# Delta rule: TensorE's program order from longer assumed times for keys, GpSimd's rows and the transposition

## The chip, the cores and the metric

The kernel runs on one core of a Trainium2 chip. The metric is the device time of one execution in microseconds, lower is better. TensorE (PE) multiplies, VectorE (DVE), ScalarE (ACT) and GpSimd (POOL) work on the vectors, and SyncE (SP) issues nearly all transfers.

## The reference

A decoder trunk of four layers on 256 tokens of width 1024. Each layer adds a mixer and a convolutional feed-forward part to the residual stream. The mixers are block attention (layers 0 and 3), a short convolution (layer 1) and a gated delta rule (layer 2, 8 heads of 128). The delta rule is what the change touches:

```python
proj = h @ w_in
qkv = silu(causal_dwconv(proj[..., :3 * d], conv_w))
q = l2norm(q) * (dh ** -0.5);  k = l2norm(k)
a_mat = where(strict, einsum('bhnid,bhnjd->bhnij', k_beta, k) * decay, 0.0)
t_mat = triangular_solve(a_mat + eye, eye)          # per head and chunk
u = t_mat @ v_beta;  w = t_mat @ (k_beta * exp(gc)[..., None])
attn = where(incl, einsum('bhnid,bhnjd->bhnij', q, k) * decay, 0.0)
def step(state, inp):
    v_new = u_i - w_i @ state
    o_i = q_i @ state + a_i @ v_new
    state = state * sd_i[..., None, None] + einsum('bhck,bhcv->bhkv', k_i, v_new)
o = rmsnorm(o) * norm_w * silu(z);  return o @ w_o
```

## The kernel before

**Weights.** All weights come in one stream of 128x1024 chunks. SyncE loads a chunk (`wraw`, L128), ScalarE rounds it (`whi`, L150), VectorE takes the remainder (`wlo`, L151). Each block of a projection is three TensorE products of 128x256, all at line L252 with an output named `mm`. The small products of the delta rule also stand at L252, their transpositions at L255, both with an output named `sm` (four PSUM banks in turn).

**The delta rule.** Projections run in the order of `GDN_FILL`: queries with keys of heads 0 to 7 (q0 to q7), then values (v0 to v3, two heads each) and gates (z0 to z3). Between them runs the work of two halves, heads 0 to 3 and heads 4 to 7. For each half: `lengths` transposes queries and keys and squares them; `systems` multiplies keys with keys and queries (`sm<-yqk`), scales the result into `aq` on VectorE (L733), and stores it to DRAM (L741); `invert` reloads its 16-row blocks (`bl`, L756), inverts them row by row on GpSimd (L764 to L769), stores the result (L771) and reloads it (`xc`, L774); VectorE spreads it (`xt`, L777) and transposes it (`xi`, L784, in `turn`); `join16` and two `join_half` put the blocks together on TensorE; `solve`, `scores` and `finish` make the output, which `output` gates and splits into two parts (L983, then ScalarE L413, VectorE L414). Then `residual` multiplies with the output weights, in the order of `PLAN_HALVES`: for all eight blocks first the part of heads 0 to 3, then that of heads 4 to 7. It needs the mark `o0` for the first and `o1` for the second.

**The order on TensorE** is written while the program is built. `Weave` counts model time: each block of a projection costs `TILE`, and each step of the small work yields its cost and how long to wait, or the marks to wait for. A step is put into TensorE's program at the first place in the projections at which its wait has passed by the model. The model delays nothing on the chip; it only decides the order. The waits that matter here:

```python
wv.set(f"q{h}", L_QK)      # queries_keys: from SiLU to the transpositions
yield 0, L_JOIN            # invert: from GpSimd's start to join16
yield 0, L_XI              # join16: behind each turn(s)
wv.set(f"o{s.h0 // G_H}", L_OUT)
```

TensorE keeps the order so written. The orders of VectorE, ScalarE, GpSimd and SyncE come out of a scheduler at build time that starts from the same program. Every engine has one static order.

Of the kernel before, what the change touches and what calls it, by code (L numbers as in the profile page):

```python
# [36 lines left out]
TILE = 0.327  # L37
LAG = 1.75
L_HEAD, L_SOFTMAX, L_TURN, L_MIX, L_READY = 3.5, 9.0, 1.0, 2.5, 0.5
L_QK, L_V, L_LEN, L_SYS, L_BLOCKS, L_JOIN, L_XI, L_PM, L_OUT = 6.0, 6.0, 1.0, 0.5, 6.0, 13.0, 1.0, 2.5, 1.0  # L40


PV_MIX = 0
# [1068 lines left out]
```

## Time and profile before

| what | value |
|---|---|
| median of 3 runs | 1251.23 us (1249.75 to 1251.76) |
| the profiled execution, its own time | 1250.79 us |
| its span, first to last instruction | 1248.8 us |
| VectorE, ScalarE, GpSimd busy | 77%, 58%, 8% |
| share of TensorE in the chain that ended last | 89% |
| mean granted TensorE clock | 0.995 |

The profiled execution is a run of its own: 2.0 us of its time lie outside the span. TensorE is busy nearly throughout, so the kernel's time is TensorE's work plus the times in which TensorE waits. The projections of the delta rule begin at about 581 us and its output projection ends at about 758 us.

### The profile page before, as it was taken

Reading aid. Unit: us, or ns where it says so; the run is one execution under the profiler, and the core shown is the slowest. Engines: PE = TensorE matmul, PEld = TensorE weight load, DVE = VectorE, ACT = ScalarE, POOL = GpSimd, SP = SyncE. Lnnn points to the kernel's source line nnn. Section 1 sums busy time; section 2 is a strip of 40 time slices with the busy share of each in tenths; the row PEclk is TensorE's granted clock in tenths of the full one; section 3 lists DMA queues with packets and bytes.
Section 4 is the critical chain, followed back from the end, with each engine's and each line's share of the span. In section 5 each row is a group of like instructions: output and inputs, shape, how many; then the busy total and the mean of one; then the engine's idle time right before and its main releaser. Section 6 shows DMA issues by size and latency. Waiting matters only on the chain.

```text
span 1248.8 us, 23934 instructions
## 1 busy us (share of the span) xinstructions
PE 1230.1 (98%) x9454; PEld 1179.2 (94%) x9454; DVE 958.5 (77%) x1588; ACT 729.7 (58%) x1259; POOL 106.1 (8%) x147
## 2 busy tenths in 40 slices
PE   9999999999999999999997999999999999999997
PEld 8989999989999999989997999999989989999986
DVE  6756999866878999866995568999675756999852
ACT  6655766644445666545873656666554655766641
POOL 2002000001002000002045102000011002000000
PEclk9999999999999999999998999999999999999998
DMA  8645555555555555555344345655655444555550
GB/s 288 200 153 168 178 182 188 185 189 194 177 182 186 184 186 186 186 186 188 125 132 124 90 136 158 199 185 186 192 189 177 156 161 164 178 186 185 186 185 34
DMA packets 67424, 215.91 MB, mean 173 GB/s; under 512 B 11248, under 2 KB 14832, under 8 KB 67312
## 3 DMA queue, kind: packets, MB, share of 16 engines
q1 hardware_dynamic: 67024, 213.86, 52.6%
q8 instruction: 74, 1.21, 0.4%
q10 hardware_dynamic: 288, 0.52, 0.1%
q14 instruction: 38, 0.31, 0.1%
HBM read 212.13 MB, written 2.23 MB: 172 GB/s over the span
## 4 chain that ended last, share of the span: by engine, by line
PE 89%; DVE 4%; ACT 2%; DMA 2%; issue 1%; POOL 1%; SPq 0%; POOLq 0%; DVEq 0%; ACTq 0%
PE mm L252 83%; PE sm L252 5%; DVE wlo L151 1%; PE sm L255 1%; DVE xl L290 1%; DVE yqk L420 1%; POOL xm L767 1%; ACT whi L150 1%; POOL xb L769 1%; DMA wraw<-wstream 1%; DMA x<-xT 0%; ACT jk L704 0%; DMA xc<-d 0%; DVE x L390 0%; DVE big L667 0%
## 5 line engine op out<-in xcount | busy, mean ns | idle before, releaser
L151 DVE TENSOR_TENSOR wlo<-wraw,whi 128x1024 fp32r<-128x1024 f32 (+1 forms) x404 | 490.0, 1213 | 186.1 <-ACT whi L150 184.3
L252 PE MATMUL mm<-xh,whi 128*128 128x256 f32 x2112 | 602.5, 285 | 0.0
L252 PE MATMUL mm<-xh,wlo 128*128 128x256 f32 x2112 | 594.7, 282 | 1.0 <-DVE wlo L151 0.9
L252 PE MATMUL mm<-xl,whi 128*128 128x256 f32 x2112 | 594.6, 282 | 0.7 <-DVE xl L290 0.7
L150 ACT CAST whi<-wraw 128x1024 fp32r<-128x1024 f32 (+1 forms) x404 | 420.1, 1040 | 290.8 <-PE mm L252 255.8
L252 PEld LDWEIGHTS mm<-xl,whi 128*128 128x128 f32 x2112 | 399.0, 189 | 1.9 <-DVE xl L290 1.1
L252 PEld LDWEIGHTS mm<-xh,wlo 128*128 128x128 f32 x2112 | 398.7, 189 | 1.7 <-DVE wlo L151 1.6
L252 PEld LDWEIGHTS mm<-xh,whi 128*128 128x128 f32 x2112 | 399.1, 189 | 1.2
L252 PE MATMUL mm<-aw,whi 128*128 128x512 f32 x704 | 247.3, 393 | 0.0
L252 PE MATMUL mm<-aw,wlo 128*128 128x256 f32 x704 | 199.1, 283 | 0.0
L252 PEld LDWEIGHTS mm<-aw,whi 128*128 128x128 f32 x704 | 132.2, 188 | 30.4
L420 DVE SCALAR_TENSOR_TENSOR y<-u,pv,y 128x255 f32<-128x255 f32 (+1 forms) x352 | 146.0, 477 | 0.0
L304 POOL TENSOR_TENSOR sq<-sq 128x256 f32<-128x256 f32 x62 | 52.9, 854 | 979.3 <-ACT sq L302 977.6
L252 PEld LDWEIGHTS mm<-aw,wlo 128*128 128x128 f32 x704 | 132.4, 188 | 0.0
L413 ACT CAST aw<-a 128x256 fp32r<-128x256 f32 x88 | 35.7, 406 | 99.8 <-DVE a L439 99.8
L418 ACT ACTIVATE y<-u,pv 128x256 f32<-128x256 f32 x176 | 79.6, 500 | 8.6 <-DVE u L432 8.6
L432 DVE TENSOR_TENSOR u<-mm,rb 128x512 f32<-128x512 f32 x88 | 60.5, 688 | 2.8 <-PE mm L252 1.3
L290 DVE SCALAR_TENSOR_TENSOR xl<-x,pv,xh 128x256 fp32r<-128x256 f32 x64 | 52.8, 856 | 3.2 <-ACT xh L289 3.2
L437 ACT ACTIVATE y<-y 128x256 f32<-128x256 f32 x88 | 36.6, 418 | 19.0 <-DVE y L420 16.9
L289 ACT ACTIVATE xh<-x,pv 128x256 fp32r<-128x256 f32 x64 | 32.1, 502 | 10.8 <-DVE x L390 6.4
L414 DVE TENSOR_TENSOR aw<-a,aw 128x256 fp32r<-128x256 f32 x88 | 36.5, 416 | 1.9 <-ACT aw L413 1.9
L302 ACT ACTIVATE sq<-x 128x256 f32<-128x256 f32 x72 | 29.1, 404 | 14.5 <-DVE x L406 14.5
(195 smaller groups left out, 1060.6 us busy)
## 6 DMA issues: line engine op xcount, KB each, us to landing
wraw<-wstream SPq DMA_DIRECT2D x396, 512.0 KB, 3.5
wraw<-wstream SPq DMA_DIRECT2D x8, 256.0 KB, 4.9
x<-xT SPq DMA_DIRECT2D x8, 128.0 KB, 4.8
d<-aq SPq DMA_DIRECT2D x2, 512.0 KB, 3.8
out<-xg ACTq DMA_DIRECT2D x2, 256.0 KB, 2.3
cs<-cst SPq DMA_DIRECT2D x1, 329.0 KB, 6.3
pv<-pvec SPq DMA_DIRECT2D x1, 324.5 KB, 5.3
cs<-cst SPq DMA_DIRECT2D x1, 320.0 KB, 4.6
```

The source lines that it names most:

```text
L150: self.nc.scalar.copy(hi[:, s], raw[:, s])
L151: self.nc.vector.tensor_sub(lo[:, s], raw[:, s], hi[:, s].bitcast(F32))
L252: self.last = nc.tensor.matmul(*a, **k)
L289: S.activation(xh[n], xn, AF.Copy, scale=col(gain + n))
L290: V.scalar_tensor_tensor(xl[n], xn, col(gain + n), xh[n].bitcast(F32), op0=ALU.mult, op1=ALU.subtract)
L304: G.tensor_add(sums[0], sums[0], sq)
L413: S.copy(dst_h, src)
L414: V.tensor_sub(dst_l, src, dst_h.bitcast(F32))
L418: S.activation(y, u, AF.Copy, scale=col(taps[0]))
L420: V.scalar_tensor_tensor(y[:, d:], u[:, :T - d], col(c), y[:, d:], op0=ALU.mult, op1=ALU.add)
L432: V.tensor_mul(u, pairs(ps), nm.rb2)
L437: S.activation(y[:, 0, :], y[:, 0, :], AF.Silu)
```

## The change

One line of constants changes. The model's time from a head's SiLU to its transposition goes from 6.0 to 7.5, that from GpSimd's start to the first join from 13.0 to 18.5, and that behind VectorE's 32x32 transposition from 1.0 to 2.0. No instruction is added or removed; the orders differ.

```diff
-L_QK, L_V, L_LEN, L_SYS, L_BLOCKS, L_JOIN, L_XI, L_PM, L_OUT = 6.0, 6.0, 1.0, 0.5, 6.0, 13.0, 1.0, 2.5, 1.0
+L_QK, L_V, L_LEN, L_SYS, L_BLOCKS, L_JOIN, L_XI, L_PM, L_OUT = 7.5, 6.0, 1.0, 0.5, 6.0, 18.5, 2.0, 2.5, 1.0
```

On TensorE the first transpositions of the keys (heads 0 to 3) move behind 12 more projection products. The first join product, `sm<-xi32`, has 66 more projection products ahead of it in the whole program than before: 18 of them stand ahead of the last `sm<-yqk` of heads 4 to 7, and behind that row there are now 60 products instead of 12.

VectorE's order around the first join, before (`xt32`, `xi32` are the spread and the transposed blocks of heads 0 to 3, `aq_7875` belongs to heads 4 to 7, `wlo_8013` comes from the weight chunk `wraw_7801`):

```order
L151 TENSOR_TENSOR wlo_7961<-wraw_7770,whi_7960 128x1024
L733 SCALAR_TENSOR_TENSOR aq_7875<-sm_7926,sk_7858,big_7230 128x256 x2
L777 TENSOR_TENSOR xt32_7759<-xc_7757,cs_71 128x256
L784 STREAM_TRANSPOSE xi32_7952<-xt32_7759 128x256
L733 SCALAR_TENSOR_TENSOR aq_7875<-sm_7946,sk_7858,big_7230 128x256 x2
L747 TENSOR_TENSOR big_7974<-aq_7875,cs_71 128x1024
L796 TENSOR_TENSOR big_7991<-sm_7982,cs_71 128x1024
L151 TENSOR_TENSOR wlo_8013<-wraw_7801,whi_8012 128x1024
```

The same place in the order of the change (`wlo_7999` is now the one from `wraw_7801`; `u` is the convolution of the second pair of value heads):

```order
L733 SCALAR_TENSOR_TENSOR aq_7893<-sm_7947,sk_7882,big_7230 128x256 x2
L151 TENSOR_TENSOR wlo_7999<-wraw_7801,whi_7998 128x1024
L733 SCALAR_TENSOR_TENSOR aq_7893<-sm_7970,sk_7882,big_7230 128x256 x2
L747 TENSOR_TENSOR big_7989<-aq_7893,cs_71 128x1024
L856 TENSOR_TENSOR u_8010<-mm_7899,rb_6997 128x512
L151 TENSOR_TENSOR wlo_8044<-wraw_7844,whi_8043 128x1024
L420 SCALAR_TENSOR_TENSOR u_8012<-u_8010,pv_70,u_8012 128x255 x2
L420 SCALAR_TENSOR_TENSOR u_8012<-u_8010,pv_70,u_8012 128x254 x2
L420 SCALAR_TENSOR_TENSOR u_8012<-u_8010,pv_70,u_8012 128x253 x2
L777 TENSOR_TENSOR xt32_7777<-xc_7775,cs_71 128x256
L151 TENSOR_TENSOR wlo_8120<-wraw_7904,whi_8119 128x1024
L784 STREAM_TRANSPOSE xi32_8041<-xt32_7777 128x256
```

L777 and L784 stood directly behind a pair of L733; now the remainders of three weight chunks, the last pair of L733, L747 and a convolution stand ahead of L784.

TensorE's order where heads 0 to 3 end, in the change (`sm_8681` takes the last transposition of heads 0 to 3, `mm_8551` is the last projection z3, `sm_8704` the first solve of heads 4 to 7, `mm_8711` the first block of the output projection, `big_8687` and `big_8688` the two parts of the output):

```order
L255 MATMUL sm_8681<-cs_71,m4_8640 128x128 x4
L252 MATMUL mm_8551<-xh_68,whi_8320 128x256
L252 MATMUL mm_8551<-xl_69,whi_8320 128x256
L252 MATMUL mm_8551<-xh_68,wlo_8321 128x256
L252 MATMUL mm_8551<-xh_68,whi_8320 128x256
L252 MATMUL mm_8551<-xl_69,whi_8320 128x256
L252 MATMUL mm_8551<-xh_68,wlo_8321 128x256
L252 MATMUL sm_8704<-big_8140,big_8499 128x128 x4
L252 MATMUL mm_8711<-big_8687,whi_8372 128x256
L252 MATMUL mm_8711<-big_8688,whi_8372 128x256
```

Before, 92 rows of projections and small products stood between that transposition and the first product of the output projection; now 7 do.

TensorE's order where heads 4 to 7 end, before (`sm_8856` takes their last transposition, `big_8593` and `big_8594` are still the output of heads 0 to 3):

```order
L252 MATMUL mm_8843<-big_8593,whi_8657 128x256
L252 MATMUL mm_8843<-big_8594,whi_8657 128x256
L252 MATMUL mm_8843<-big_8593,wlo_8658 128x256
L255 MATMUL sm_8856<-cs_71,m4_8804 128x128 x4
L252 MATMUL mm_8843<-big_8593,whi_8657 128x256
L252 MATMUL mm_8843<-big_8594,whi_8657 128x256
```

And in the change (`sm_8905` takes their last transposition, `big_8911` and `big_8912` are the output of heads 4 to 7):

```order
L252 MATMUL mm_8863<-big_8687,whi_8648 128x256
L252 MATMUL mm_8863<-big_8688,whi_8648 128x256
L252 MATMUL mm_8863<-big_8687,wlo_8649 128x256
L255 MATMUL sm_8905<-cs_71,m4_8891 128x128 x4
L252 MATMUL mm_8711<-big_8911,whi_8712 128x256
L252 MATMUL mm_8711<-big_8912,whi_8712 128x256
L252 MATMUL mm_8711<-big_8911,wlo_8713 128x256
```

The output projection has 96 products on heads 0 to 3 and 96 on heads 4 to 7. Before, 54 of the first 96 stood between the last scores of heads 4 to 7 (`sm<-m4,aq`) and that transposition, and 42 behind it. Now 66 of them stand ahead of those scores, 30 between, and none behind the transposition.

## Rows read from the trace of the kernel before

**Rows 1.** The page: the span, and TensorE's line of part 1 (busy us, share of the span, instructions).

```profile
span 1248.8 us, 23934 instructions
PE 1230.1 (98%) x9454; PEld 1179.2 (94%) x9454; DVE 958.5 (77%) x1588; ACT 729.7 (58%) x1259; POOL 106.1 (8%) x147
```

**Rows 2.** Who waited for whom, TensorE alone, between 600 and 840 us (the delta rule lies in it): waiting engine, tile and line, then what it waited for: us in total, times, longest.

```profile
PE sm L252 <- DVE xi L784: 5.4, 2, 4.9
```

**Rows 3.** The timeline of TensorE around the first join: start us, us, engine, line, operation, out<-in, shapes, count, and in brackets the idle time before it with its releaser.

```profile
626.41 0.66 PE L255 MATMUL sm<-cs,yqk 128*128 128x128 f32 x4 [1.03 <-ACT yqk L682]
632.79 0.66 PE L255 MATMUL sm<-cs,yqk 128*128 128x128 f32 x4 [0.30 <-ACT jk L704]
...
658.64 1.02 PE L252 MATMUL sm<-yqk 128*128 128x256 f32 x4
...
660.80 0.28 PE L252 MATMUL mm<-xh,wlo 128*128 128x256 f32 x1
665.97 3.57 PE L252 MATMUL sm<-xi,big 128*128 128x16 f32 x16 [4.88 <-DVE xi L784]
669.37 0.56 PE L252 MATMUL mm<-xh,whi 128*128 128x256 f32 x1
```

**Rows 4.** Short stretches around the first join, TensorE alone: from:to, length, TensorE's busy us (instructions), granted TensorE clock as a share of 2.4 GHz, DMA share, GB/s.

```profile
665.00:665.50 0.50, 0.00 (x0) 0.93 0.88 270
665.50:666.00 0.50, 0.03 (x1) 0.50 1.00 377
672.00:672.50 0.50, 0.50 (x5) 0.74 0.00 0
```

**Rows 5.** The same view of a stretch of the feed-forward layer behind, in which TensorE runs projection products (128x256) and nothing else.

```profile
820.00:860.00 40.00, 40.00 (x340) 1.00 0.56 185
```

**Rows 6.** The timelines of SyncE (SPq), ScalarE (ACT) and VectorE (DVE) around the first join, columns as in rows 3.

```profile
659.16 0.49 SPq L771 DMA_DIRECT2D d<-xb  x1
659.76 0.52 SPq L128 DMA_DIRECT2D wraw<-wstream  x1
...
663.69 1.04 ACT L150 CAST whi<-wraw 128x1024 fp32r<-128x1024 f32 x1 [5.42 <-DMA wraw<-wstream]
...
664.91 0.43 DVE L777 TENSOR_TENSOR xt<-xc,cs 128x256 f32<-128x256 f32 x1 [5.39 <-DMA xc<-d]
665.37 0.45 DVE L784 STREAM_TRANSPOSE xi<-xt 128x256 f32<-128x256 f32 x1
665.74 0.83 DVE L733 SCALAR_TENSOR_TENSOR aq<-sm,sk,big 128x256 f32<-128x256 f32 x2
666.61 1.23 DVE L747 TENSOR_TENSOR big<-aq,cs 128x1024 f32<-128x1024 f32 x1
```

**Rows 7.** The timeline of GpSimd (POOL): the first and the last operation of its block of 28 multiplies and subtractions, for the first half of the heads and for the second.

```profile
642.42 0.73 POOL L764 TENSOR_SCALAR xb<-bl 64x15 f32<-64x15 f32 x1 [8.88 <-DMA bl<-d]
...
658.89 0.24 POOL L769 TENSOR_TENSOR xb<-xb,xm 64x15 f32<-64x15 f32 x1
...
674.36 0.26 POOL L764 TENSOR_SCALAR xb<-bl 64x15 f32<-64x15 f32 x1 [9.43 <-DMA bl<-d]
...
688.21 0.24 POOL L769 TENSOR_TENSOR xb<-xb,xm 64x15 f32<-64x15 f32 x1
```

**Rows 8.** Groups of VectorE's instructions by line between 600 and 800 us: busy us, mean ns of one, then idle us before them.

```profile
L151 DVE TENSOR_TENSOR wlo<-wraw,whi 128x1024 fp32r<-128x1024 f32 x49 | 59.9, 1224 | 5.2 <-ACT whi L150 5.1
L420 DVE SCALAR_TENSOR_TENSOR u<-u,pv 128x255 f32<-128x255 f32 (+2 forms) x24 | 10.4, 497 | 0.3 <-ACT u L418 0.3
L856 DVE TENSOR_TENSOR u<-mm,rb 128x512 f32<-128x512 f32 x4 | 2.7, 678 | 4.2 <-PE mm L252 4.2
```

**Rows 9.** The timeline of TensorE behind the first join, columns as in rows 3.

```profile
677.48 1.07 PE L252 MATMUL sm<-xi,aq 32*32 32x32 f32 x32 [0.54 <-DVE xi L784]
...
682.73 0.69 PE L252 MATMUL sm<-xt,m 32*32 32x32 f32 x16 [0.84 <-ACT big L841]
```

**Rows 10.** The end of a half of the heads, from several engines' timelines: for heads 0 to 3 the last transposition and the first two conversions of the output; for heads 4 to 7 the last scores and the product behind them, the scaled output, the transposition and the conversions.

```profile
718.40 0.60 PE L255 MATMUL sm<-cs,m 128*128 128x128 f32 x4
...
720.58 1.15 ACT L413 CAST big<-z 128x512 fp32r<-128x512 f32 x2
...
722.12 1.29 DVE L414 TENSOR_TENSOR big<-z,big 128x512 fp32r<-128x512 f32 x2
...
733.86 1.05 PE L252 MATMUL sm<-m,aq 128*128 128x128 f32 x8
734.66 0.48 PE L252 MATMUL mm<-big,whi 128*128 128x256 f32 x2
...
739.42 0.69 DVE L906 TENSOR_TENSOR m<-m,f 128x512 f32<-128x512 f32 x1
...
741.05 0.60 PE L255 MATMUL sm<-cs,m 128*128 128x128 f32 x4
...
743.44 0.62 ACT L413 CAST big<-z 128x512 fp32r<-128x512 f32 x1 [1.16 <-DVE z L983]
...
744.09 0.69 DVE L414 TENSOR_TENSOR big<-z,big 128x512 fp32r<-128x512 f32 x1
```

**Rows 11.** The last two waits of the kernel: TensorE's timeline, and the short stretch in which the clock falls (columns as in rows 4).

```profile
1240.18 0.61 PE L252 MATMUL sm<-cs,sq 128*128 128x1 f32 x4 [1.14 <-ACT sq L302]
...
1242.00:1243.00 1.00, 0.79 (x4) 0.64 0.00 0
```

## The prediction

> **What bounds the kernel now.** I read the page first: TensorE is busy 1230.1 of 1248.8 us [rows 1]. The change neither adds nor removes an instruction, so it can move the time only through TensorE's waits and its clock. The view of waits, cut to the delta rule, comes next: one wait stands out, 4.9 us for `xi` of L784 [rows 2]. Then I read the timeline around that wait. TensorE ends its last projection product at 660.80 + 0.28 = 661.08 and starts the first join at 665.97 [rows 3]. The clock follows: in the stretch from 665.0 to 665.5 the mean is 0.93, then 0.50, and 0.74 from 672.0 to 672.5 [rows 4]. With the two levels 2.4 and 1.2 GHz that is a fall at 665.43, 4.35 us into the wait, and a rise at 672.26. Of these 6.8 us, 0.5 were idle and 6.3 were work at half clock, which cost 3.15 us. So the first join costs 4.88 + 3.15 = 8.0 us.
>
> What is late there? GpSimd ends its rows at 658.89 + 0.24 = 659.13 [rows 7]; SyncE's store starts at 659.16, and the next weight chunk is issued only behind it, at 659.76 [rows 6]. The reload lets L777 run at 664.91, L784 at 665.37. ScalarE gets the chunk at 663.69, after 5.42 us without one. Note VectorE's order: a pair of L733 runs at 665.74, behind L777, though its products began at 658.64 and took 1.02 us [rows 3, 6]. It stood behind an instruction that waited 5.39 us for a transfer. VectorE here keeps its written order.
>
> **Step 1, the keys 1.5 later.** The transpositions of heads 0 to 3 get 12 more products ahead. A product costs 40.00/340 = 0.118 us [rows 5], so that is 1.4 us, more than the 1.03 us waited for the SiLU. But the second wait, 0.30 us, is for ScalarE's squares [rows 3], and the systems come just as close behind the transpositions as before. I take these waits as moved, not removed: 0, between -1.3 (both gone) and +1.0 (the pace of ScalarE shows again at each system).
>
> **Step 2, the first join.** TensorE comes to it 66 products later: 66 x 0.118 = 7.8, at 668.9. If `xi` were still ready at 665.9 the wait would be gone. But VectorE's new order puts ahead of L784 the remainder of the very chunk (`wraw_7801`) whose load stands behind the store. ScalarE's cast of it starts at 663.69 and ends at 664.73 [rows 6]. From there VectorE has, with its own rows: L151 1.22, the pair of L733 0.83, L747 1.23, L856 0.68, L151 1.22, six L420 of 0.50, L777 0.43, L151 1.22, L784 0.45 [rows 6, 8], together 10.3 us. Instructions in a row overlap somewhat (two L733 take 0.83, L777 and L784 start 0.46 apart), so I take a tenth off: 9.3, `xi` at 674.0. TensorE then waits 674.1 - 668.9 = 5.2 us instead of 4.88: +0.3. What makes the first join late is then no longer GpSimd's rows but VectorE's place for L777.
>
> The bounds: GpSimd's block took 659.13 - 642.42 = 16.7 us for the first half and 688.45 - 674.36 = 14.1 us for the second [rows 7], the same 28 operations. With the shorter one all behind it comes 2.6 us sooner: a wait of 2.6. At the other end, without the overlap, 6.2; the load can land later by another 0.6.
>
> The clock falls again at 4.35 us into the wait: 0.85 us idle, 6.0 us of work at half clock, 3.0 us instead of 3.15: -0.2. If the wait stays under 4.35 us, the fall is saved, -3.15.
>
> The Trainium skill ("PSUM — Partial Sum Buffer", section "Engine vs sequencer instructions") says that the queues of ScalarE, VectorE and GpSimd are strictly first in, first out; by it L777 can't pass the waiting L151, and the row at 665.74 agrees. If it could pass, the sum would lose the 5.2 and 3.0 us of the new stall.
>
> **Step 3, behind the join.** L_XI puts 24 products instead of 12 ahead of the 32-row join, which covers the 0.54 us waited for the second `xi` [rows 9]. The 0.84 us for a ScalarE copy stays in the same pattern but with the copies in another order; I take half. Together -0.9, between 0 and -1.4.
>
> **Step 4, the end of the halves.** The work now comes later, but the projections that cover it end where they did. Three places lose cover.
> (a) Output of heads 0 to 3. Before, 92 rows stand between its transposition and the output projection; now 7. In the trace the transposition starts at 718.40, the first rounded half is ready at 720.58 + 0.60 = 721.2 (half of the pair's 1.15), the remainder at 722.12 + 0.69 = 722.8 [rows 10], 2.8 and 4.4 us later. In the new order L970 (a product like L856, 0.68) stands ahead of L414 where the trace has an L151 of 1.22: 3.9. Now TensorE has the transposition 0.36, six products 0.71 and a solve (0.80, as the scores from 733.86 to 734.66): 1.9. It waits 0.9, then, a product later, 1.0: +1.9.
> (b) Last scores to transposition of heads 4 to 7: the scores start at 733.86, the scaled output ends at 739.42 + 0.69 = 740.11: 6.25 us [rows 10]. Cover: scores 0.80 and 30 products 3.55. Before it was 54 products and no wait. +1.9.
> (c) Transposition to the second half of the output projection. 741.05 to 743.44 + 0.62 = 744.06 and to 744.09 + 0.69 = 744.78 [rows 10]: 3.0 and 3.7 us. Before, 42 products (4.95 us) hid it; now nothing but the transposition, 0.36, and one product: +3.2.
> Together +7.0. I bound it by 5.5 (VectorE and ScalarE have fewer weight chunks between) and 8.
>
> **Step 5, the rest.** The second join comes 7.8 us later too, while its chain grows by the pair's place on VectorE and one more load ahead of its reload on SyncE, whose issue costs 0.5 us [rows 6]; I take 0. Weights: TensorE's 48 products more ahead of the join use chunks converted before SyncE's block, so none is waited for.
>
> **Sum**: 0 + 0.3 - 0.2 - 0.9 + 7.0 = +6.2. The profiled execution took 1250.79, its span and 2.0 us around it, and lies 0.4 under the median of 1251.23, within the runs' own spread of 2.0; I leave that difference out: 1257.0.
>
> **Rivals.**
> - *The clock falls at the end as well.* Waits (b) and (c) lie close together with little work between, 5.1 us waited in all. For it: at the kernel's end two waits of 1.1 us with a few small products between were enough, the clock fell there at 1242.28 (mean 0.64 over the stretch from 1242.0) [rows 11]. Against it: in the first join 4.35 us of full idleness were needed. It would cost about what it did, 3.15 us: 1260.1. The Trainium skill ("Perfetto Trace Analysis", section "Matmul Optimizations") says that TensorE's power follows its use and that products should therefore be issued back to back in batches; by it the fall is likely, and the row at 1242 agrees while no row shows this very pattern. Chance 0.2.
> - *The first join's wait becomes shorter than the fall of the clock*, by GpSimd's shorter block or earlier loads: 2.6 to 4.2 us waited, no half clock. 6.2 - 1.0 - 3.0 = +2.2 to 6.2 - 2.6 - 3.0 = +0.6: 1251.4 to 1253.0. Chance 0.13.
> - *It ends faster*: `xi` is ready when TensorE comes, the whole 8.0 us go. Place: L777 on VectorE; it decides when L784 ends before 668.9, 5 us sooner than worked out. Then 0 - 8.0 - 0.9 + 7.0 = -1.9: 1248.9 or below, if step 4 is over-sized. Against it: the rows in order ahead of L777. Chance 0.07.
> - *Nothing at the end*: if the outputs were ready at their places, 6.2 - 7.0 = -0.8: 1250.0, no change. Against it: three chains read row by row. Chance 0.04.
>
> **How the numbers follow.** The likeliest, stall moved and cover lost, has 0.56: 1257.0. Within 0.2% (2.5 us, about what a measurement of this kernel can tell from no change) lie most of the second rival (0.11), the fourth (0.04) and a little of the third (0.02); faster is the rest of the third. Slower 0.78, same 0.17, faster 0.05. The range goes from 1252.3, inside the second rival, to 1260.5, above the first.
>
> **What would show it.** In the changed profile: a wait of TensorE for `xi` of L784 of about 5 us at 669 to 674 instead of 661 to 666; L777 behind six L420 on VectorE; a clock at 0.5 behind it; new waits of TensorE at `mm<-big` for L413 and L414 (near 2 and 3 us) and before the last transposition for L906 (near 2). Wrong would be: no such wait at the end, or an `xi` ready by 669.

## The result, and the profile after

The changed kernel takes 1261.04 us (median of 4 runs, 1259.85 to 1261.37), the kernel before 1250.92 on the same chip: ratio 1.0076, 95% interval 1.0064 to 1.0089, or +10.1 us by the medians. Forecast were +6.2 and 1257.0; the time lies 0.5 us above the top of the range. It is slower, as forecast, by more than forecast.

TensorE's line on the page of the changed kernel, whose span is 1257.8 us (before: [rows 1]), and the view of TensorE's waits from 600 to 840 us (before: [rows 2]):

```profile
PE 1233.1 (98%) x9454; PEld 1180.7 (94%) x9454; DVE 959.0 (76%) x1588; ACT 729.4 (58%) x1259; POOL 104.4 (8%) x147
```

```profile
PE sm L252 <- DVE xi L784: 6.7, 1, 6.7
PE mm L252 <- ACT big L413: 2.8, 2, 2.1
PE sm L255 <- DVE m L906: 2.5, 1, 2.5
PE mm L252 <- DVE big L414: 0.7, 1, 0.7
```

The wait for `xi` is longer, not shorter, and three waits at the end of the halves (L413, L906, L414) are new.

How much is waiting and how much clock shows best over the whole delta rule: from a small product at 589 us, ahead of which both orders are the same, to the first wait of the next layer (762.53 us before, 771.74 after). One row for each kernel, before first; columns from:to, length, TensorE's busy us (instructions), granted clock, DMA share, GB/s:

```profile
589.06:762.53 173.47, 165.46 (x1486) 0.98 0.40 125
```

```profile
589.04:771.74 182.70, 168.88 (x1487) 0.95 0.37 118
```

The stretch is 9.23 us longer; the two profiled executions differ by 1259.85 - 1250.79 = 9.06 us, so all of it is here. TensorE is idle 182.70 - 168.88 = 13.82 instead of 8.01 us: +5.8 of waiting. It is busy 3.4 us longer with the same products. Not all of that is the clock, as the rows on the clock below show.

TensorE's timeline after, at the places of [rows 3] and [rows 10]:

```profile
630.24 1.13 PE L252 MATMUL sm<-yqk 128*128 128x256 f32 x4 [0.39 <-ACT jk L704]
634.53 0.63 PE L255 MATMUL sm<-cs,yqk 128*128 128x128 f32 x4 [0.17 <-DVE aq L733]
...
668.21 0.28 PE L252 MATMUL mm<-xh,wlo 128*128 128x256 f32 x1
675.17 1.01 PE L252 MATMUL sm<-xi,big 128*128 128x16 f32 x4 [6.69 <-DVE xi L784]
...
729.71 0.39 PE L252 MATMUL mm<-big,whi 128*128 128x256 f32 x1 [0.65 <-ACT big L413]
730.79 0.39 PE L252 MATMUL mm<-big,whi 128*128 128x256 f32 x1 [0.69 <-DVE big L414]
...
750.43 1.12 PE L255 MATMUL sm<-cs,m 128*128 128x128 f32 x4 [2.49 <-DVE m L906]
753.66 1.30 PE L252 MATMUL mm<-big,whi 128*128 128x256 f32 x2 [2.11 <-ACT big L413]
```

TensorE comes to the first join at 668.21 + 0.28 = 668.5 and gets `xi` at 675.17. The waits of [rows 9] (0.54 and 0.84) are gone. At the end it waits 0.65 + 0.69 + 2.49 + 2.11 = 5.94 us where it waited nothing.

The clock, in short stretches of TensorE's view (columns as in [rows 4]):

```profile
671.00:672.00 1.00, 0.00 (x0) 0.86 1.19 328
681.00:682.00 1.00, 1.00 (x7) 0.52 0.00 0
...
750.00:751.00 1.00, 0.57 (x3) 0.62 0.10 41
757.00:758.00 1.00, 1.00 (x10) 0.97 0.00 0
...
671.73:681.97 10.24, 6.79 (x32) 0.50 0.46 127
750.23:757.06 6.83, 4.37 (x17) 0.50 0.22 79
```

A mean of 0.86 is a fall to 1.2 GHz at 671.72, 3.2 us into the wait (before: 4.35), and the clock stays low until 681.96, 10.2 us instead of 6.8. A second stretch, 750.24 to 757.06, lies at the end of the halves, where before there was none.

The last two rows give the work that TensorE did in the low stretches: 6.79 + 4.37 = 11.2 us, against 6.3 in the kernel before. An estimate from these rows, with half of such work lost: the clock cost 5.6 us instead of 3.1, which is 2.4 more (0.2 at the first join, 2.2 at the end). That leaves 1.0 of the 3.4 us. It goes with the order itself: the same subtraction over the delta rule gives 163.3 us of work at full clock here and 163.2 in e5 and e9, which have this order, but 162.3 in the kernel before and 161.8 in e6, which has its order, and in e10, with that order and no fall, 162.06 us are read directly. What in the order costs it isn't shown.

And the chain to `xi`: first SyncE in the kernel before, in a stretch ahead of [rows 6], then the timelines of SyncE, GpSimd, ScalarE and VectorE after (before: [rows 6, 7]):

```profile
636.68 0.38 SPq L741 DMA_DIRECT2D d<-aq  x1
639.63 0.69 SPq L756 DMA_DIRECT2D bl<-d  x1
```

```profile
637.68 0.38 SPq L741 DMA_DIRECT2D d<-aq  x1
642.01 0.70 SPq L756 DMA_DIRECT2D bl<-d  x1
...
660.37 0.49 SPq L771 DMA_DIRECT2D d<-xb  x1
660.99 0.51 SPq L128 DMA_DIRECT2D wraw<-wstream  x1
```

```profile
645.09 0.26 POOL L764 TENSOR_SCALAR xb<-bl 64x15 f32<-64x15 f32 x1 [9.61 <-DMA bl<-d]
...
660.11 0.24 POOL L769 TENSOR_TENSOR xb<-xb,xm 64x15 f32<-64x15 f32 x1
```

```profile
664.74 1.05 ACT L150 CAST whi<-wraw 128x1024 fp32r<-128x1024 f32 x1 [7.62 <-DMA wraw<-wstream]
```

```profile
665.83 1.23 DVE L151 TENSOR_TENSOR wlo<-wraw,whi 128x1024 fp32r<-128x1024 f32 x1 [5.81 <-ACT whi L150]
...
673.12 0.42 DVE L777 TENSOR_TENSOR xt<-xc,cs 128x256 f32<-128x256 f32 x1
...
674.59 0.44 DVE L784 STREAM_TRANSPOSE xi<-xt 128x256 f32<-128x256 f32 x1
```

From VectorE's L151 at 665.83 to the end of L784 at 675.03 it is 9.2 us, the chain worked out as 9.3. It only began 1.1 us later than taken: ScalarE's cast came at 664.74, not 663.69. GpSimd had started at 645.09, not 642.42 [rows 7], because SyncE issued `bl` 2.4 us later (642.01 against 639.63).

### The profile page after: what moved, and what is told of

Its sections match the earlier page's. It is cut to its first block, busy times and chain, and to the rows that moved or that the text cites. A ratio compares the mean times of both kernels' runs of the same rounds, so it can differ in the third digit from the quotient of the medians.

```text
span 1257.8 us, 23928 instructions
## 1 busy us (share of the span) xinstructions
PE 1233.1 (98%) x9454; PEld 1180.7 (94%) x9454; DVE 959.0 (76%) x1588; ACT 729.4 (58%) x1259; POOL 104.4 (8%) x147
## 4 chain that ended last, share of the span: by engine, by line
PE 90%; DVE 4%; ACT 2%; DMA 2%; issue 2%; POOL 1%; SPq 0%; POOLq 0%; DVEq 0%; ACTq 0%
PE mm L252 84%; PE sm L252 5%; DVE wlo L151 1%; PE sm L255 1%; DMA wraw<-wstream 1%; DVE xl L290 1%; ACT whi L150 1%; POOL xm L767 1%; POOL xb L769 0%; ACT jk L704 0%; DMA d<-aq 0%; DVE x L390 0%; DMA x<-xT 0%; DMA bl<-d 0%; DVE z L983 0%
## 5 line engine op out<-in xcount | busy, mean ns | idle before, releaser
L151 DVE TENSOR_TENSOR wlo<-wraw,whi 128x1024 fp32r<-128x1024 f32 (+1 forms) x404 | 490.5, 1215 | 196.8 <-ACT whi L150 195.2
L420 DVE SCALAR_TENSOR_TENSOR y<-u,pv,y 128x255 f32<-128x255 f32 (+1 forms) x352 | 146.0, 477 | 0.0
L413 ACT CAST aw<-a 128x256 fp32r<-128x256 f32 x88 | 35.7, 406 | 99.4 <-DVE a L439 99.4
L437 ACT ACTIVATE y<-y 128x256 f32<-128x256 f32 x88 | 36.6, 418 | 18.9 <-DVE y L420 16.7
L289 ACT ACTIVATE xh<-x,pv 128x256 fp32r<-128x256 f32 x64 | 32.1, 502 | 11.2 <-DVE x L390 6.3
L414 DVE TENSOR_TENSOR aw<-a,aw 128x256 fp32r<-128x256 f32 x88 | 36.4, 415 | 1.9 <-ACT aw L413 1.9
```

The source lines that it names most:

```text
L151: self.nc.vector.tensor_sub(lo[:, s], raw[:, s], hi[:, s].bitcast(F32))
L289: S.activation(xh[n], xn, AF.Copy, scale=col(gain + n))
L413: S.copy(dst_h, src)
L414: V.tensor_sub(dst_l, src, dst_h.bitcast(F32))
L420: V.scalar_tensor_tensor(y[:, d:], u[:, :T - d], col(c), y[:, d:], op0=ALU.mult, op1=ALU.add)
L437: S.activation(y[:, 0, :], y[:, 0, :], AF.Silu)
```

## The experiments

Four questions: are the three times separate? Does L777's place on VectorE make the stall, or the late chunk? What does the clock cost? What remains when GpSimd's rows are short? Ratios are to the kernel before on the same chip, with the 95% interval; 0.001 is 1.25 us.

**One time alone.** Three kernels, each the kernel before with one constant changed:

```diff
-L_QK = 6.0
+L_QK = 7.5      # e1_keys
-L_JOIN = 13.0
+L_JOIN = 18.5   # e2_join
-L_XI = 1.0
+L_XI = 2.0      # e3_turn
```

> The kernel before with only the keys' time changed (L_QK 7.5). Theory P (the place on VectorE decides: the stall comes from the place of L777 and L784 behind the remainder of a weight chunk that SyncE loads late): 0 to +3 us. Six products more stand ahead of the first join, but L784 now stands behind the remainder of chunk wraw_7801, so xi comes near 667 and TensorE, there at about 662, waits 5 to 6 us instead of 4.9; the two early waits for squared keys (1.03 and 0.30) go. Theory J (the join's time alone makes the change slow, the keys' time is free): -1.3 to 0, 1249.6 to 1250.9, xi's wait as before.

> The kernel before with only the join's time changed (L_JOIN 18.5). Theory P: L777 stands behind the remainders of two late chunks, as in the changed kernel; TensorE comes at about 666.5 to the join and waits 5 to 7 us for xi; together with lost cover in the last third of the delta rule +5 to +9, 1256 to 1260. Theory J: the whole +10.1 of the changed kernel is here, 1259 to 1262. If TensorE only needed the 5.5 us that the time gives it (a rival), xi is ready and the time falls to about 1243 to 1246.

> The kernel before with only the transposition's time changed (L_XI 2.0). L777 keeps its place on VectorE; 12 products more (1.42 us) stand ahead of the first join and of each later one. Theory P: TensorE waits 4.88 - 1.42 = 3.5 us for xi; that is shorter than the 4.35 us after which the clock fell before, so the half clock (3.15 us) and the second join's 0.54 go: -4 to -5, 1246 to 1247, if nothing later waits. Rival: the later joins now stand ahead of VectorE's backlog and the waits move there: 1250 to 1256. Theory J: 1249.5 to 1251.

Measured: keys alone 1262.36 us, 1.0086 (1.0073 to 1.0099); join alone 1262.64, 1.0091 (1.0078 to 1.0104); transposition alone 1254.97, 1.0020 (1.0009 to 1.0031). The three add up to 1.0197, the whole change is 1.0076: they are not separate costs. (The executions of e1 differ with the clock: the two shortest, 1258.2 and 1258.5 us, had a mean granted clock of 0.991, the other four, 1262.3 to 1264.2 us, one of 0.986 or 0.987. The profiled one is the shortest, so the rows below show less of what the clock cost than the median holds. Those of e3 lie between 1250.9 and 1256.9, the profiled one at 1254.97.) TensorE's timeline of e1_keys, and its clock in the stretches around the first of these waits:

```profile
667.37 0.80 PE L252 MATMUL sm<-xi,big 128*128 128x16 f32 x3 [6.87 <-DVE xi L784]
...
682.72 1.27 PE L252 MATMUL sm<-xi,aq 32*32 32x32 f32 x32 [3.06 <-DVE xi L784]
```

```profile
662.00:663.00 1.00, 0.00 (x0) 0.95 0.96 348
676.00:677.00 1.00, 1.00 (x10) 0.73 0.00 0
```

`xi` comes at 667.4, near the 667 of theory P, since L784 stands behind the late remainder. But the clock was low from 662.9 to 676.5, twice as long as in the kernel before, and a second wait of 3.06 us came behind; P's +3 was far too little, and J, by which the keys are free, falls. e2_join alone, at 1262.64, came out 0.6 us above J's range and 2.6 above P's, so neither theory holds for both. There is next to no wait at the end of the halves here (the longest 0.56 us); the waits are at the joins. In e2_join they are as in the changed kernel: 7.36 us for `xi`, then 2.01 for L906 and 1.54 + 1.23 for the output.

In e3_turn TensorE waited 3.60 us, as P said (3.5), and yet the clock fell:

```profile
665.25 0.92 PE L252 MATMUL sm<-xi,big 128*128 128x16 f32 x7 [3.60 <-DVE xi L784]
...
693.72 0.48 PE L252 MATMUL sm<-xi,big 128*128 128x16 f32 x3 [3.01 <-DVE xi L784]
```

```profile
666.00:667.00 1.00, 1.00 (x11) 0.97 0.90 358
670.00:671.00 1.00, 1.00 (x9) 0.82 0.91 372
```

It fell at 666.9, 1.7 us after work had begun again, and rose at 670.4; it fell a second time, from 694.2 to 701.1. The 1.3 us gained at the first join came back as 3.01 us at the second half's and 1.75 for L906: the rival of this run is right.

**L777 early, TensorE's order as in the changed kernel.**

```diff
+L_SPREAD = 13.0
 ...
-                yield 0, L_JOIN
+                yield 0, L_SPREAD
 ...
                 turn(s)
-                yield 0, L_XI
+                yield 0, L_JOIN - L_SPREAD + L_XI
```

> The changed kernel with its whole order on TensorE kept up to the second half's join, but L777 and L784 of each half are handed over 13.0 after GpSimd's start, as before, and only the join's products wait for 18.5 and 2.0 more. L777 stands ahead of the late chunk's remainder again and L784 behind it, eight rows sooner than in the changed kernel. Theory P: xi is ready by about 668, TensorE comes at 668.5, so no wait at the first join and no half clock: -6.7 - 3.4 = -10 at that place, 1251 to 1253 with the tail unchanged. Rival (backlog): VectorE stands still from about 659 to 666 for SyncE's late load whatever stands first in its order, so the stall only passes to the next product that needs VectorE, the transposition of values a few products behind the join: a wait of 3 to 5 us there, 1256 to 1260.

1258.32 us, 1.0052 (1.0040 to 1.0064). VectorE's and TensorE's timelines:

```profile
664.99 0.42 DVE L777 TENSOR_TENSOR xt<-xc,cs 128x256 f32<-128x256 f32 x1 [6.04 <-DMA xc<-d]
...
666.47 0.44 DVE L784 STREAM_TRANSPOSE xi<-xt 128x256 f32<-128x256 f32 x1
```

```profile
667.26 1.85 PE L252 MATMUL sm<-xi,big 128*128 128x16 f32 x16
...
673.80 1.12 PE L255 MATMUL sm<-cs,u 128*128 128x128 f32 x4 [3.88 <-ACT u L860]
```

`xi` was ready at 666.9 and the first join ran without a wait at 667.26. So L777's place does set the wait for `xi`. But VectorE still stood 6.04 us, now for `xc`, and TensorE waited 3.88 us for the values a few products later. The backlog theory names the place and the time right. The time is not that of this place alone: behind the second half's join the order is another than in the changed kernel, with waits of 1.42 us there and of 3.15 for L413 at the end.

**Store and reload on GpSimd's queue,** so that no weight chunk stands behind them on SyncE, in the changed kernel and in the one before:

```diff
-                nc.sync.dma_start(out=d2..., in_=xb)
+                nc.gpsimd.dma_start(out=d2..., in_=xb)
 ...
-                    nc.sync.dma_start(out=xc, in_=d2...)
+                    nc.gpsimd.dma_start(out=xc, in_=d2...)
```

> The changed kernel with the store d<-xb and the reload xc<-d issued by GpSimd instead of SyncE, so that the load of the next weight chunk no longer stands behind a store that waits for GpSimd's rows. Orders of TensorE and VectorE as in the changed kernel. Theory B (backlog: SyncE stands still for the store until about 660, so VectorE and ScalarE stand still from about 659 to 666 for the chunk that comes late, and all they owe TensorE comes late): no such stillness; L777 and L784 end near 667, TensorE comes at 668.5: no wait, no half clock, -6.7 - 3.4 = -10 at the first join, with the end of the halves as it is 1250 to 1252. Rival (the chain from GpSimd's last row to xi is the limit, or the transfers issued by GpSimd are slower): a wait of 3 to 7 us stays, 1256 to 1262.

> The same in the kernel before: store and reload issued by GpSimd, all orders of the compute engines as before. Theory B: xc lands as before, but the rows behind L784 on VectorE find their chunk there; xi itself waits for GpSimd's rows, whose end does not move, so the first wait becomes 3 to 4.9 us; under 4.35 us the clock stays, which gives back 3.15: 1246 to 1251. Rival (transfers issued by GpSimd take longer than those by SyncE): xi later by their difference, 1252 to 1256.

Changed kernel 1257.2 us, 1.0040 (1.0027 to 1.0053); kernel before 1253.3, 1.0008 (0.9999 to 1.0017). From the timelines of e5_queue_after:

```profile
665.58 0.94 POOL L774 DMA_DIRECT2D xc<-d  x1 [3.61 <-DMA d<-xb]
```

```profile
669.15 0.43 DVE L777 TENSOR_TENSOR xt<-xc,cs 128x256 f32<-128x256 f32 x1 [2.49 <-DMA xc<-d]
```

```profile
671.21 1.12 PE L252 MATMUL sm<-xi,big 128*128 128x16 f32 x7 [3.72 <-DVE xi L784]
```

The stillness of VectorE went (no gap over 0.3 us ahead of L777 but this one), and the wait fell from 6.69 to 3.72 us: the late chunk was worth 3 us of waiting. The clock gave nothing back: the low stretch behind the wait was shorter (6.8 instead of 10.2 us), but TensorE worked in all of it, 6.8 us at half clock as in the changed kernel. The rest is the transfers themselves: GpSimd waited 3.61 us for its store, where SyncE's reload followed the store in 2.0 us (662.35 behind 660.37 in the changed kernel). The rival's range holds. In the kernel before, where no chunk stood ahead of L777, nothing was won: TensorE waited 5.57 us, and theory B's 1246 to 1251 is missed.

**Idle products for the clock.** Zeros multiplied right ahead of the first join, 16 in the changed kernel (e7), 12 in the kernel before (e8):

```diff
+                if s.h0 == 0:
+                    keep_busy = bank("sm")
+                    for _ in range(16):
+                        PE.matmul(keep_busy[:, :T], lhsT=idle[:, :P], rhs=idle, start=True, stop=True)
                 pp = bank("sm")
```

> The changed kernel with 16 idle products (128x256 of zeros, about 0.43 us each by the ten at the kernel's start, 6.9 us) on TensorE right ahead of the first join's products of heads 0 to 3, where it waits 6.7 us. They use nothing that is late. Theory C (clock): the stall itself stays, but TensorE is busy in it, so its clock does not fall: -3.4 + 0.2, 1257 to 1259. If the half clock behind the stall costs nothing: 1261.

> The kernel before with 12 such idle products (5.2 us) ahead of the first join's products of heads 0 to 3, where it waits 4.88 us. Theory C: no half clock behind, -3.15 + 0.3: 1247.5 to 1248.5. If the half clock costs nothing: 1251 to 1252.

The changed kernel went from 1261.04 to 1257.12, 1.0047 (1.0035 to 1.0060), as expected. Here the stall's clock, from the view of short stretches:

```profile
668.00:676.00 8.00, 7.81 (x42) 1.00 0.74 240
```

TensorE is no sooner done (`xi` comes at 674.94), but its clock stays full, and that alone is worth 3.6 us by the ratios (1.0076 to 1.0047). The kernel before gained nothing that can be told from no change: 1250.53, 0.9993 (0.9984 to 1.0002). Its timeline and clock:

```profile
666.13 1.04 PE L252 MATMUL sm<-xi,big 128*128 128x16 f32 x8 [0.18 <-DVE xi L784]
...
694.03 1.15 PE L252 MATMUL sm<-xi,big 128*128 128x16 f32 x9 [2.48 <-DVE xi L784]
```

```profile
696.00:697.00 1.00, 1.00 (x7) 0.57 0.80 328
```

The first join is clean; but TensorE now comes to the second half's join earlier than its `xi`, waits 2.48 us where the kernel before did not wait, and loses its clock there. Time won at the first half is given back at the second, whose GpSimd rows start when they did (674.13 against 674.36 [rows 7]).

Two more runs, with idle products at a second place as well: in e11 six ahead of the last transposition of the changed kernel, in e12 five ahead of the second half's join of the kernel before.

> The changed kernel with the 16 idle products ahead of the first join (1257.1 before) and 6 more, about 2.6 us, ahead of the last transposition of heads 4 to 7, where TensorE waits 2.49 us. Theory C: the second fall of the clock (6.8 us low from 750) goes as well: -2 to -3, 1254 to 1255.5. If the fall at the end costs nothing, or comes a little later in the wait of 2.1 us that follows: 1257.

> The kernel before with the 12 idle products ahead of the first join (1250.5 before) and 5 more, about 2.1 us, ahead of the second half's, where TensorE then waited 2.48 us and its clock fell at 696.4 for 3.3 us. Theory C: that fall goes, -1.6 + 0.1: 1248.5 to 1249.5, the fastest of all. Otherwise 1250.5.

e11: 1257.75 us, 1.0052 (1.0039 to 1.0065), nothing won over e7. The fall only moved on: `big` of L413 was still 2.11 us late, and behind that wait, which ended at 751.48, the clock fell at 751.7 for 3.4 us. In the profiled execution `xi` also came later than in e7 (GpSimd began at 645.56, there at 644.52), so that TensorE waited 1.58 us behind its idle products instead of 0.19; this run therefore doesn't price the fall at the end. In e12 the fall did not go either: with no wait left but one of 0.28 us, which ended at 706.45, the clock fell at 708.3 for 3.4 us, amid the second half's small products. e12: 1249.77, 0.9992 (0.9981 to 1.0002), the lowest median of the kernels that leave nothing out, but not to be told from the kernel before.

**Half of GpSimd's rows,** in both kernels, which leaves out part of the inverse:

```diff
-                for k in range(1, BLK - 1):
+                for k in range(1, BLK - 1, 2):
```

> The changed kernel with every second of GpSimd's 14 steps of the 16x16 inversion left out (7 pairs of L767 and L769 instead of 14), in both halves; all orders as in the changed kernel. It leaves out part of the inverse. Theory G (GpSimd's rows, the store behind them and what SyncE and VectorE then owe are the chain that sets the stall in both kernels; the change only put TensorE's wait at another place of it, and took cover from the end): store at about 652 instead of 660, no chunk late, xi ready when TensorE comes at 668.5; -6.7 - 3.4; the waits at the end of the halves (5.9) and their half clock stay: 1250 to 1252. Rival (VectorE's own rows ahead of L777 are the limit): a wait of over 2 us for xi stays.

> The same rows left out in the kernel before. Theory G: xi is ready at about 659 to 661, no wait and no half clock at the first join, the second half's rows also earlier: -4.9 - 3.15, 1242 to 1244. The difference of the two kernels with half of the rows is then the cover lost at the end alone, +6 to +8. If the end's waits came from GpSimd's rows too, the two would be equal.

The changed kernel: 1253.72 us, 1.0019 (1.0009 to 1.0028), above the 1250 to 1252 expected. The kernel before: 1243.57, 0.9942 (0.9929 to 0.9956), as expected. The whole stretch of the delta rule, kernel before and then changed kernel, and the changed kernel's waits:

```profile
588.63:753.70 165.07, 162.06 (x1487) 1.00 0.40 131
```

```profile
589.14:765.98 176.84, 168.66 (x1487) 0.96 0.39 122
```

```profile
669.76 1.48 PE L252 MATMUL sm<-xi,big 128*128 128x16 f32 x12 [1.17 <-DVE xi L784]
...
743.47 1.11 PE L255 MATMUL sm<-cs,m 128*128 128x128 f32 x4 [2.48 <-DVE m L906]
746.70 0.58 PE L252 MATMUL mm<-big,whi 128*128 128x256 f32 x1 [2.11 <-ACT big L413]
```

With its GpSimd block at 8 to 9 us the kernel before loses the first stall but for 0.45 us: no wait over 1.1 us is left, the clock does not fall in this stretch, and the 8 us of the first join are gone. The changed kernel keeps 1.17 us of its 6.69. Both gain about the same, and the difference between them stays what it was: 1.0019 - 0.9942 = 0.0077. So most of the difference does not come from the first join. What differs with short rows are the same four waits at the end of the halves as in the changed kernel (5.93 us in all), the clock behind them and behind the 1.17 us, and the 1.1 us by which the changed order needs more at full clock (163.2 against 162.06): 8.18 us idle against 3.01, 168.66 us busy against 162.06. (The profiled execution of the changed kernel took 1255.35, 1.6 us over its median.) The +6 to +8 expected had no half clock at the end in them; by the ratios it is 9.6 us. The kernel before with half of the rows also measures what the clock cost in the kernel before: 162.06 us is what TensorE needs in that order at full clock, so half clock cost 165.46 - 162.06 = 3.4 us there.

## Why the prediction was right, and where its sizes were off

Right: the direction and its two reasons. The stall at the first join moved with the join instead of going away, and the work put later lost its cover at the end. e4 shows the first (with L777 early the wait for `xi` goes), e9 and e10, with the waits in their rows, the second; no run gave the changed kernel's end its cover back. Its main case left out the second fall of the clock, and the first rival, that the clock falls at the end as well, is what happened. That the sum came within 3 us is in part luck: steps 1, 3 and 4 came out 2.4 us below their forecast, which hides part of what the other terms missed.

Step by step, against the profile after:

| step | forecast | measured |
|---|---|---|
| 1, keys' waits | 0 | 0.39 + 0.17 instead of 1.33: -0.8 |
| 2, wait for `xi` | +0.3 (5.2 us) | +1.8 (6.69 us) |
| 2, clock at the first join | -0.2 | +0.2 |
| first rival, clock at the end | not in the sum (3.15 in the rival) | +2.2 |
| work at full clock | not in the sum | +1.0 |
| 3, behind the join | -0.9 | -1.4 |
| 4, end of the halves | +7.0 | +5.9 |
| sum | +6.2 | +8.9 of 9.2 |

**Step 1** took the keys' time as something that concerns keys only. The waits there were removed, not moved, and TensorE's products for them came later: the last pair of L733 let the store `d<-aq` go at 637.68 instead of 636.68, `bl` was issued 4.33 us behind it instead of 2.95, and GpSimd started 2.7 us later. Step 2 had no term for that, but for 0.6 us by which the load could land later. Why the store took 1.4 us more is not settled.

**Step 2** got the mechanism and the length of VectorE's chain (9.3 against 9.2). The start of the chain was mis-sized: GpSimd's block began 2.7 us later and was 1.45 us shorter (645.09 to 660.35), so that the chunk came 1.1 us later, and TensorE came 0.4 us sooner than worked out. That is the 1.5 us. The sentence that "what makes the first join late is then no longer GpSimd's rows but VectorE's place for L777" is half right: e4 and e9 show that both have to go. With L777 early the values are late; with short rows and L777 late 1.17 us remain.

**The clock** is the term that failed, by 2.6 us the largest miss. The forecast took 4.35 us, one reading, as the wait that it takes. The runs show falls from 2.4 us into a wait (e1) to 1.7 us behind the end of one of 3.6 us (e3), one 0.7 us into a wait of 3.88 (e4, at 670.6, behind the first join's small products), one 1.6 us behind a wait of only 1.17 (e9), and low stretches of 3.4 us (the first of e3), 6.8 (the kernel before), 10.2 (the changed kernel) and 13.6 (the first of e1). So -0.2 at the first join had no basis but that one reading, and the sentence that with a wait "under 4.35 us, the fall is saved" had none either: e3 and e5 waited 3.60 and 3.72 us and lost the clock all the same. The first rival's mechanism, with the measured 750.24 to 757.06, costs 4.4 us of work at half clock, 2.2 us, rather than 3.15; with the 0.2 at the first join the clock cost 2.4 us more in all than before.

**Work at full clock.** The prediction set out from the premise that the change can move the time only through TensorE's waits and its clock. The rows don't bear that out: by the estimate above, the same products in the other order needed about 1.0 us more at full clock.

**Step 4**: (a) 1.34 for 1.9, (b) 2.49 for 1.9, (c) 2.11 for 3.2. The places and the releasers (L413, L414, L906) are those named; the sum is 1.1 us too high.

What stays open is when exactly the clock falls, what in the order costs the 1.0 us, and 0.3 us of the sum.

## What to carry to other kernels

A consumer put later in one engine's written order can drag its producer along in another's: look where the producer lands, and behind whose late load, before counting the cover. Work that is put later at the start of a stage is missing at the stage's end; price that end with its waits and with the clock behind them. A stall that can't be removed is cheaper when TensorE does idle products in it (3.6 us in e7), but time won there counts only up to the next thing that is late (in e8 3 us were expected, and none can be told from no change).

## What the runs showed of the hardware

GpSimd's rows stretch when VectorE takes the remainder of a chunk. The timelines of VectorE and of GpSimd in the kernel before:

```profile
648.98 1.21 DVE L151 TENSOR_TENSOR wlo<-wraw,whi 128x1024 fp32r<-128x1024 f32 x1
```

```profile
649.06 1.30 POOL L767 TENSOR_TENSOR xm<-xb,bl 64x63 f32<-64x63 f32 x1
650.43 0.37 POOL L769 TENSOR_TENSOR xb<-xb,xm 64x63 f32<-64x63 f32 x1
```

The row at 649.06 lasts until L151 has ended; its neighbour with as many elements takes 0.37 us. Five L151 fall into that block of 16.7 us, each with a row of 1.13 to 1.31 us behind its start. The second block has four rows that long, three beside an L151 and one beside L813 (128x1024 as well). In e5's second half no L151 starts in the block, and the same 28 rows took 11.0 us; L796, as long as L151, does start there, but one of its inputs is `sm`, in PSUM, and the rows beside it took 0.30 us. The long rows are most of why the two blocks of [rows 7] differ by 2.6 us, which the prediction could only bound. The Trainium skill ("GPSIMD Engine Reference", section "1. Specifications") says that GpSimd's interfaces to SBUF are shared with VectorE and contend with VectorE instructions that have two inputs in SBUF; L151, with `wraw` and `whi`, is one, and the rows agree. Beside L420, whose two tensors lie in SBUF as well, rows of 64x63 and 64x64 took only 0.37 to 0.38 us, so not every such instruction holds a row up for its own length.
